# A macaron block on one core: PSUM split into whole-width and small banks, seeds written by ScalarE, and another order at the FFNs' entries

## The chip, the cores and the metric

One core of a Trainium2 chip runs the kernel, in one launch. The metric is the device time of the execution in microseconds; lower is better. The kernel before took 1777.3 us (median of 1776.07, 1777.52 and 1777.30).

Its engines, by the short names of the profile: PE (TensorE) multiplies and accumulates into PSUM, eight banks of 128 x 512 fp32; DVE (VectorE) and ACT (ScalarE) do elementwise work; SP (SyncE) issues the weight loads; POOL (GpSimd) does next to nothing here.

## What is computed

A decoder block on 256 rows of width 2048: half a SwiGLU FFN (hidden width 5632), a token mixer, another half FFN, all fp32, each behind an RMS norm.

```python
x = x + 0.5 * swiglu_ffn(rms_norm(x, ffn1_norm), ffn1_w_gate, ffn1_w_up, ffn1_w_down)
z = rms_norm(x, mix_norm) @ w_in              # 2048 -> 5120
...                                           # y: gated recurrence, gated short convolution
x = x + y @ w_out
x = x + 0.5 * swiglu_ffn(rms_norm(x, ffn2_norm), ffn2_w_gate, ffn2_w_up, ffn2_w_down)
return rms_norm(x, final_norm)

def swiglu_ffn(x, w_gate, w_up, w_down):
    return (silu(x @ w_gate) * (x @ w_up)) @ w_down
```

## The kernel before

Weights come from HBM in units of 512 x 512 (1 MB, `raw_*`, three buffers). For fp32 accuracy each unit is split in two: `hi` is an ACT cast (two of 128x1024), `lo` the DVE difference of raw and hi (one of 128x2048). Activations are split alike. A product then takes three matmuls for each pair of 128-row tile and 128-deep slice: hi by hi and hi by the activation's lo (one group), then the weight's lo by the activation's hi. A unit against one 128-row tile is 12 matmuls of 128x512.

**Order.** A tile scheduler orders each engine's instructions by priorities and dependences; only the opening and the last product are pinned to program order. Each engine runs its queue in that order, and an instruction that waits holds up all that are behind it on its engine.

**The FFN** (`ffn`). The first 512 columns of gate and up are plain products over four units (names `ps_g`, `ps_u`; in FFN1 the gate's is `opening`, made while x arrives). The squares of x are summed meanwhile; `factor` then makes the row factor `r`, and `rows` spreads it: `diag_n` (identity by r) is multiplied by ones into bank `pb_n`, twice, and copied to `bc_n`. Gate and up of the first columns are scaled by r when evicted. For the other columns the normalised activations themselves are made: `v` is hi + lo of the transposed x, times `bc_n`, and is split again into `x` (hi, lo). Sums and differences of its quarters (`seven_of`) give the split `xs`.

The other 5120 columns run as five pairs of gate and up, each a Strassen-Winograd form (`seven`): seven products of half size in place of eight, with one more stream of usual products accumulated in the same banks. A seven has four banks, `a`, `c`, `e` and `d`. Its start: product 0 into `a`, ACT copies `a` to SBUF (`s1`); product 4 into `c`, ACT copies `c` to SBUF (`s5`); then usual products into `e` (fresh) and `c`; product 5 goes on in `a`, and so on. At the end DVE adds the kept copies to the banks, four adds, and the results are `u3`, `u2`, `a` and `s1`. The matmuls of a seven with two streams are 180. Its raw units w11 and w12 are in the `kept` buffers, two, which the two `v` tiles use before them.

After pairs 0, 2 and 4 the hidden units made so far are transposed on PE (`ph`, in `turn_hidden`, called by `settle`), split by ACT (hi) and DVE (lo), some copied back by ACT, and multiplied by the down weights: columns 0 and 3 as plain products (`ps_d`), columns 1 and 2 as a seven. DVE adds half of each result to `xres`, the residual, in SBUF.

**The mixer** projects by w_in (`columns`, `ps_in`), runs the two branches, and projects back by w_out (`ps_o`); DVE adds the result, times a row factor, to `xres`.

**PSUM.** One pool of eight banks serves everything in turn.

**Queues.** SP issues all weight loads in order; a load waits until its buffer is free.

Of the kernel before, what the change touches and what calls it, by code (L numbers as in the profile page):

```python
# [10 lines left out]
F32 = mybir.dt.float32  # L11
# [16 lines left out]
EPS = 1e-6  # L28
SQRT_FLOOR = 2.0**-114


# [17 lines left out]
def hybrid_block(ctx: ExitStack, tc: tile.TileContext, a: dict, out: bass.AP):  # L49
# [28 lines left out]
    work = ctx.enter_context(tc.tile_pool(name="work", bufs=2))  # L78
    psum = ctx.enter_context(tc.tile_pool(name="psum", bufs=8, space=bass.MemoryType.PSUM))

    def bank(name):
        return psum.tile([P, 512], F32, tag="ps", name=name)

# [13 lines left out]
    ones = const.tile([P, P], F32, name="ones")  # L97
    dve.memset(ones, 1.0)
    vec = {}

    def load_vectors(group, name, engine):
        n = sum(g[2] for g in group)
        rows = const.tile([n, P], F32, name=f"rows_{name}")
        cols = const.tile([P, n], F32, name=f"cols_{name}")
        at = 0
        for key, ap, k in group:
            engine.dma_start(rows[at : at + k, :], ap.rearrange("(r p) -> r p", p=P))
            vec[key] = cols[:, at : at + k]
            at += k

        def turn():
            pv = bank(f"pv_{name}")
            pe.transpose(pv[:, :n], rows, ident[:n, :n])
            dve.tensor_copy(cols, pv[:, :n])

        return turn

    first_turn = load_vectors([("ffn1_norm", a["ffn1_norm"][0], 16)], "first", nc.sync)
    load_x(0)
# [87 lines left out]
    class Norm:  # L207
# [12 lines left out]
        def turn(self, ks):  # L220
            for k in ks:
                pt = bank(f"pt_{self.name}_{k}")[:, :S]
# [20 lines left out]
        def rows(self):  # L243

            pb = bank(f"pb_{self.name}")
# [39 lines left out]

    def product(w, c, us, y, name, stagger=False, between=None):
        ps = [bank(f"ps_{name}_{t}") for t in range(NT)]
        cs = slice(c * CW, (c + 1) * CW)
        late = []
        for i, u in enumerate(us):  # L290
            blk = unit(w[u * UK * P : (u + 1) * UK * P, cs], f"{name}_{u}")
            begin, end = i == 0, i == len(us) - 1
            if stagger and i >= len(us) - 2:
                late.append((u, blk, begin, end))
            else:
                multiply([(ps[t], stationary(y(u), t), begin, end) for t in range(NT)], blk)
            if between:
                between(i)
            pump(1.5)
        for t in range(NT):  # L300
            for u, blk, begin, end in late:
                multiply([(ps[t], stationary(y(u), t), begin, end)], blk)
        return ps
# [22 lines left out]
    def seven(w, rows, c0, sf, xs, name, keep, between=None):  # L326
# [50 lines left out]
        product_of(1, w21, d)  # L377
        dve.tensor_tensor(u3, u3, s5, op=ALU.add)
        dve.tensor_tensor(u3, e, u3, op=ALU.add)
        dve.tensor_tensor(u2, c, u2, op=ALU.add)  # L380
        dve.tensor_tensor(s1, d, s1, op=ALU.add)
        return {(1, 1): u3, (0, 1): u2, (1, 0): a, (0, 0): s1}

    def ffn(tag, norm, after, opening=None):
        with tc.tile_pool(name=f"ffn{tag}", bufs=1) as fp:
# [40 lines left out]
            norm.factor()  # L426
            norm.rows()
            sg = [keep(f"sg{tag}_0_{t}") for t in range(NT)]
# [5 lines left out]
            vs = [vs[u // 2][:, :, u % 2, :] for u in range(4)]  # L434
            bcs = norm.bc.unsqueeze(1).to_broadcast([P, UK, S])
            xs = []
            for u in range(4):
                x = f32(norm.xT[u])
# [5 lines left out]
                if u == 1:  # L444
                    pair = [big(f"xs{tag}_{i}") for i in range(2)]
                    sf = seven_of(
                        xs[0], xs[1], {(t, i): vs[i][:, :, t * P : (t + 1) * P] for t in range(NT) for i in range(2)},
                        quad(keep(f"spare{tag}")),
                        [(b[:, :, o : o + P], b[:, :, o + P : o + S]) for b in pair for o in (0, S)],
                    )  # L450
# [9 lines left out]
            def down(last):  # L460
                us = sorted(set(hidden) | {w[0] for w in waiting})

                def update(c, t, ps):
                    xr = xres[:, t, c * CW : (c + 1) * CW]
                    Engine.pinned = last and tag == 2 and c == NC_D - 1
                    dve.scalar_tensor_tensor(xr, ps, 0.5, xr, op0=ALU.mult, op1=ALU.add)
                    if last:
                        after(c, t)

                for c in (0, 3):  # L470
                    end = last and tag == 2 and c == NC_D - 1
                    ps = product(
                        wd, c, us, hidden.get, f"d{tag}_{us[0]}_{c}", end, (lambda i: settle()) if c == 0 else None
                    )
                    for t in range(NT):
                        update(c, t, ps[t])
                    if c == 0:
# [8 lines left out]
                        for c1 in (1, 2):  # L486
                            for t in range(NT):
                                update(c1, t, q[t, c1 - 1])
                hidden.clear()
                turned.clear()  # L490

            for s in range(5):
                c0 = CW + 2 * s * CW
                g = seven(wg, (0, 1), c0, sf, xs, f"g{tag}_{s}", keep, settle)
                for q in ((1, 1), (0, 1), (1, 0), (0, 0)):
                    if q == (1, 0):
                        z = keep(f"z{tag}_{s}")
                        act.activation(z, g[q], AF.Silu)
                        g[q] = z
                    else:  # L500
                        act.activation(g[q], g[q], AF.Silu)
                h = seven(wu, (0, 1), c0, sf, xs, f"u{tag}_{s}", keep)
                for t, n in ((1, 1), (0, 1), (1, 0), (0, 0)):
                    dve.tensor_tensor(g[t, n], h[t, n], g[t, n], op=ALU.mult)
                    waiting.append((1 + 2 * s + n, t, g[t, n], s % 2 == 0))
# [4 lines left out]

    def small(name):
        return const.tile([P, NH], F32, name=name)

    sp2, hba, hbi = small("sp2"), small("hba"), small("hbi")

    def prepare():
# [3 lines left out]
        lam = vec["lru_lambda"]  # L520
        m, e, den, sr, s2, pl = (small(f"lam_{n}") for n in ("abs", "exp", "den", "s", "s2", "poly"))
        act.activation(m, lam, AF.Abs)
# [19 lines left out]
    def opening(wg):  # L542

        ps = [bank(f"ps_g1_0_{t}") for t in range(NT)]
        for u in range(KD // UK):
# [5 lines left out]
            else:  # L551
                blk = unit(src, f"g1_0_{u}")
            for j in range(UK):
# [28 lines left out]

    with tc.tile_pool(name="mixer", bufs=1) as mp, tc.tile_pool(name="mixw", bufs=2) as mw:
        wgate = {}
# [37 lines left out]
        def gates(q):  # L622
# [5 lines left out]
            for g, hb in (("a", hba), ("i", hbi)):  # L628
                hi, lo = wgate[g]
                pg = bank(f"pgate_{g}_{q}")  # L630
                pe.matmul(pg[:, :S], hi[:, q, :], xs[:, :S], start=True, stop=False)
# [149 lines left out]
        for c in range(NC_D):  # L781
            cs = slice(c * CW, (c + 1) * CW)
            for g in range(2):
# [3 lines left out]
                if c == 0:  # L787
                    pst = bank(f"pst_{g}")
                    for t in range(NT):
# [57 lines left out]

    ffn(2, n2, last)

# [29 lines left out]
```

## Time and profile before

| | us |
|---|---|
| median of three runs | 1777.30 |
| profiled execution | 1779.27 |
| its span (first to last instruction) | 1777.3 |
| mean granted clock of PE | 0.994 |

| stage | from about (us) | to about (us) |
|---|---|---|
| FFN1, start to the first seven | 0 | 72 |
| FFN1, sevens and down products | 72 | 736 |
| mixer | 736 | 1059 |
| FFN2, start to the first seven | 1059 | 1109 |
| FFN2, sevens, down products and end | 1109 | 1777 |

How to read the profile: its page has the busy time of each engine. A view of waits sums, for each engine, the idle time before an instruction by what ended it. A timeline lists groups of like instructions by start, with their length, engine, tiles (out <- in), count (xN) and, in brackets, the idle time before them and what ended it. A view of windows has, for each stretch, its length, the busy time of each engine, the granted clock, the share of DMA and GB/s. Names lack buffer numbers: `ps_g` is any of several. All helper calls stand at line 42. Records of matmuls are pipelined: their pitch from start to start, not their length, is what PE needs for one.

### The profile page before, as it was taken

How to read it: one execution, taken by the hardware profiler on the slowest of the kernel's cores; microseconds unless marked ns; L12 is line 12 of the kernel's file. 1: busy time of each engine (PE TensorE's matmuls, PEld its weight loads, DVE VectorE, ACT ScalarE, POOL GpSimd, SP SyncE). 2: the span in 40 equal slices, each digit the busy share in tenths (PEclk: the TensorE clock that was granted, in tenths of full speed). 3: DMA queues.
4: the chain of work that ended last, by engine and by line, in shares of the span. 5: the costliest groups of instructions: out<-in, count | busy, mean ns of one | idle time of the engine just before them, and what ended most of it. 6: DMA issues, size and time to landing. Idle time of an engine off the chain costs nothing. (4 is left out here: it accounts for less than half of the span.)

```text
span 1777.3 us, 20302 instructions
## 1 busy us (share of the span) xinstructions
PE 1744.6 (98%) x8031; PEld 1441.5 (81%) x8031; DVE 1494.4 (84%) x1221; ACT 1046.8 (59%) x1342; POOL 6.9 (0%) x32
## 2 busy tenths in 40 slices
PE   7999999999999999999999999999999999999998
PEld 5787888888888888888888887887888888888886
DVE  6898989989789888688987667989899887899895
ACT  6565556656465656575765554656566664556664
POOL 1000000000000000000000000000000000000000
PEclk9999999999999999999999999999999999999999
DMA  7366655574566574456565655574566637555743
GB/s 249 132 214 212 213 189 190 190 245 155 186 196 209 172 256 166 145 188 196 175 196 170 209 189 190 190 242 157 192 214 202 209 135 259 189 190 190 257 158 106
DMA packets 173905, 343.24 MB, mean 193 GB/s; under 512 B 5621, under 2 KB 8049, under 8 KB 173681
## 3 DMA queue, kind: packets, MB, share of 16 engines
q1 hardware_dynamic: 173344, 340.82, 57.2%
q8 instruction: 63, 1.03, 0.2%
q10 hardware_dynamic: 144, 1.05, 0.2%
q14 instruction: 34, 0.27, 0.0%
q0 software_dynamic: 320, 0.07, 0.0%
HBM read 339.82 MB, written 2.10 MB: 192 GB/s over the span
## 5 line engine op out<-in xcount | busy, mean ns | idle before, releaser
L42 PE MATMUL ps_in<-xT_nm,hi_in 128*128 128x512 f32 x640 | 224.1, 395 | 0.0
L42 ACT CAST hi_g_p<-raw_g 128x1024 fp32r<-128x1024 f32 x140 | 140.5, 1048 | 123.4 <-DVE raw_g L42 40.9
L42 DVE TENSOR_TENSOR lo_g_p<-raw_g,hi_g_p 128x2048 fp32r<-128x2048 f32 x70 | 159.7, 2287 | 36.0 <-ACT hi_g_p L42 35.5
L42 ACT CAST hi_u_p<-raw_u 128x1024 fp32r<-128x1024 f32 x140 | 141.5, 1049 | 66.3 <-PE ps_u_a L42 25.9
L42 PE MATMUL ps_in<-xT_nm,lo_in 128*128 128x256 f32 x640 | 178.6, 281 | 0.6 <-DVE lo_in L42 0.6
L42 DVE TENSOR_TENSOR lo_u_p<-raw_u,hi_u_p 128x2048 fp32r<-128x2048 f32 x70 | 159.2, 2286 | 22.2 <-ACT hi_u_p L42 22.1
L42 PE MATMUL ps_d<-hi_d,h 128*128 128x512 f32 x704 | 172.2, 396 | 2.8 <-DVE h L42 2.2
L42 PEld LDWEIGHTS ps_d<-hi_d,h 128*128 128x128 f32 x704 | 132.6, 189 | 33.3 <-DVE h L42 3.0
L42 PEld LDWEIGHTS ps_in<-xT_nm,hi_in 128*128 128x128 f32 x640 | 119.8, 187 | 27.1
L42 ACT CAST hi_d<-raw_d 128x1024 fp32r<-128x1024 f32 x88 | 88.0, 1048 | 81.9 <-PE ps_u_d L42 25.3
L42 DVE TENSOR_TENSOR lo_d<-raw_d,hi_d 128x2048 fp32r<-128x2048 f32 x44 | 100.7, 2289 | 31.7 <-ACT hi_d L42 31.7
L42 PEld LDWEIGHTS ps_in<-xT_nm,lo_in 128*128 128x128 f32 x640 | 120.6, 189 | 1.4 <-DVE lo_in L42 1.1
L42 DVE TENSOR_TENSOR lo_in<-raw_in,hi_in 128x2048 fp32r<-128x2048 f32 x40 | 91.4, 2285 | 32.7 <-ACT hi_in L42 32.5
L42 ACT CAST hi_in<-raw_in 128x1024 fp32r<-128x1024 f32 x80 | 81.5, 1049 | 62.1 <-PE ps_in L42 48.8
L42 ACT CAST hi_d_p<-raw_d 128x1024 fp32r<-128x1024 f32 x84 | 84.5, 1048 | 48.2 <-DVE raw_d L42 21.0
L42 DVE TENSOR_TENSOR lo_d_p<-raw_d,hi_d_p 128x2048 fp32r<-128x2048 f32 x42 | 95.5, 2287 | 18.9 <-ACT hi_d_p L42 18.8
L42 ACT CAST hi_g_x<-raw_g 128x1024 fp32r<-128x1024 f32 x80 | 80.8, 1049 | 41.2 <-PE ps_g_c L42 19.9
L42 ACT CAST hi_u_x<-raw_u 128x1024 fp32r<-128x1024 f32 x80 | 80.6, 1049 | 37.3 <-PE ps_u_c L42 25.8
L42 DVE TENSOR_TENSOR raw_u<-raw_u,raw_u 128x2048 f32<-128x2048 f32 x40 | 91.6, 2291 | 9.4 <-DMA raw_u<-in_ffn_w_up_dram 8.7
L42 DVE TENSOR_TENSOR raw_g<-raw_g,raw_g 128x2048 f32<-128x2048 f32 x40 | 91.5, 2287 | 6.4 <-DMA raw_g<-in_ffn_w_gate_dram 5.8
L42 DVE TENSOR_TENSOR lo_g_x<-raw_g,hi_g_x 128x2048 fp32r<-128x2048 f32 x40 | 91.4, 2286 | 3.8 <-ACT hi_g_x L42 3.7
L42 DVE TENSOR_TENSOR lo_u_x<-raw_u,hi_u_x 128x2048 fp32r<-128x2048 f32 x40 | 91.5, 2287 | 3.7 <-ACT hi_u_x L42 3.1
(349 smaller groups left out, 3612.5 us busy)
## 6 DMA issues: line engine op xcount, KB each, us to landing
raw_u<-in_ffn_w_up_dram SPq DMA_DIRECT2D x88, 1024.0 KB, 5.3
raw_d<-in_ffn_w_down_dram SPq DMA_DIRECT2D x88, 1024.0 KB, 5.1
raw_g<-in_ffn_w_gate_dram SPq DMA_DIRECT2D x87, 1024.0 KB, 5.3
raw_in<-in_w_in_dram SPq DMA_DIRECT2D x40, 1024.0 KB, 5.1
raw_o<-in_w_out_dram SPq DMA_DIRECT2D x16, 1024.0 KB, 5.1
xres<-in_x_dram SPq DMA_DIRECT2D x4, 512.0 KB, 8.3
fin<-in_final_norm_dram ACTq DMA_DIRECT2D x1, 1024.0 KB, 4.7
out_dram<-xres SPq DMA_DIRECT2D x4, 256.0 KB, 2.7
```

Of the source, the lines that this page charges most:

```text
L42: ins = getattr(self.engine, name)(*args, **kwargs)
```

## The change

- PSUM: in each FFN six banks ("full") for products and two ("part") for transposes and other small results; all eight in the mixer for both. The pools are opened for FFN1, the mixer and FFN2 in turn, over the same banks. When an FFN's pools are opened, six matmuls on zeros write the six full banks (`first_*`).
- Sevens: after product 0 ACT copies `a` to bank `d`, and after product 4 `c` to bank `e`; the later products accumulate on them, with no start flag. Two of four DVE adds go; the other two are made where the result is used.
- Down products, columns 0 and 3 (all but the very last): ACT writes twice the residual into the bank first, the matmuls accumulate on it, and ACT writes half of the bank to `xres`.
- Opening: units 1 to 3 of FFN1's first product have their lo made in two halves.
- Row factor: `rows` and the normalising of unit u are called from within the up product (`between=normalise`), after its unit u, and not ahead of that product.

```diff
+    zeros = const.tile([P, 512], F32R, name="zeros")
+    dve.memset(f32(zeros), 0.0)
...
+    def banks(name, parts):
+        with ExitStack() as st:
+            for kind, n in (("full", 8 - parts), ("part", parts)):
+                if n:
+                    pools[kind] = st.enter_context(
+                        tc.tile_pool(name=f"{kind}_{name}", bufs=n, space=bass.MemoryType.PSUM)
+                    )
+            if parts:
+                for i in range(8 - parts):
+                    pe.matmul(bank(f"first_{name}_{i}"), zeros[:, :P], zeros, start=True, stop=True)
+            else:
+                pools["part"] = pools["full"]
+            yield
...
+    def small(name):
+        return bank(name, "part")
...
-    def product(w, c, us, y, name, stagger=False, between=None):
+    def product(w, c, us, y, name, stagger=False, between=None, base=None):
         ps = [bank(f"ps_{name}_{t}") for t in range(NT)]
+        if base:
+            for t in range(NT):
+                act.activation(ps[t], base(t), AF.Copy, scale=2.0)
...
-            begin, end = i == 0, i == len(us) - 1
+            begin, end = i == 0 and not base, i == len(us) - 1
...
         product_of(0, w11, a, True)
-        s1 = snap(a, "s1")
+        act.copy(d, a)
         dve.tensor_tensor(w11, w12, w11, op=ALU.subtract)
         product_of(4, w11, c, True)
-        s5 = snap(c, "s5")
-        usual(0, b2, 1, (e, 1, True, not two), (c, 0, False, False))
+        act.copy(e, c)
+        usual(0, b2, 1, (e, 1, False, not two), (c, 0, False, False))
...
-        usual(0, a2, 0, (d, 0, True, False), (a, 1, False, False))
+        usual(0, a2, 0, (d, 0, False, False), (a, 1, False, False))
...
-        dve.tensor_tensor(u3, u3, s5, op=ALU.add)
-        dve.tensor_tensor(u3, e, u3, op=ALU.add)
-        dve.tensor_tensor(u2, c, u2, op=ALU.add)
-        dve.tensor_tensor(s1, d, s1, op=ALU.add)
-        return {(1, 1): u3, (0, 1): u2, (1, 0): a, (0, 0): s1}
+        return {(1, 1): (e, u3), (0, 1): (c, u2), (1, 0): (a, None), (0, 0): (d, None)}
...
-                pt = bank(f"ph{tag}_{u}_{t}")
+                pt = small(f"ph{tag}_{u}_{t}")
...
             norm.factor()
-            norm.rows()
...
-            for u in range(4):
+
+            def normalise(u):
+                if u == 0:
+                    norm.rows()
+                bcs = norm.bc.unsqueeze(1).to_broadcast([P, UK, S])
                 x = f32(norm.xT[u])
                 dve.tensor_tensor(vs[u], x[:, :, :S], x[:, :, S:], op=ALU.add)
                 dve.tensor_tensor(vs[u], vs[u], bcs, op=ALU.mult)
...
+            pu = product(wu, 0, range(4), norm.xT.__getitem__, f"u{tag}_0", between=normalise)
             xs = list(enumerate(xs))[2:]
-            pu = product(wu, 0, range(4), norm.xT.__getitem__, f"u{tag}_0")
...
                     ps = product(
-                        wd, c, us, hidden.get, f"d{tag}_{us[0]}_{c}", end, (lambda i: settle()) if c == 0 else None
+                        wd, c, us, hidden.get, f"d{tag}_{us[0]}_{c}", end, (lambda i: settle()) if c == 0 else None,
+                        None if end else lambda t: columns_of(c, t),
                     )
...
+                        xr = columns_of(c, t)
+                        if end:
+                            Engine.pinned = True
+                            dve.scalar_tensor_tensor(xr, ps[t], 0.5, xr, op0=ALU.mult, op1=ALU.add)
+                        else:
+                            act.activation(xr, ps[t], AF.Copy, scale=0.5)
...
-                blk = unit(src, f"g1_0_{u}")
+                halves_of = ((0, 2), (2, 4))
+                blk = parts_of(load(src, f"g1_0_{u}"), f"g1_0_{u}", halves_of, lambda i: None)
...
+    ffn1_banks.close()
-    with tc.tile_pool(name="mixer", bufs=1) as mp, tc.tile_pool(name="mixw", bufs=2) as mw:
+    with tc.tile_pool(name="mixer", bufs=1) as mp, tc.tile_pool(name="mixw", bufs=2) as mw, banks("mixer", 0):
...
-    ffn(2, n2, last)
+    with banks("ffn2", 2):
+        ffn(2, n2, last)
```

In a seven, the gate's and up's epilogues add `e` to `u3` and `c` to `u2` on DVE and read `a` and `d` from PSUM directly; in the down product the two parts are added to `xres` one after the other.

More of the change, by code (lines that the diff above doesn't have):

```diff
@@ L2 @@
 from collections import deque
-from contextlib import ExitStack
+from contextlib import ExitStack, contextmanager
 import concourse.bass as bass
@@ L29 @@
 SQRT_FLOOR = 2.0**-114
+QUADS = ((1, 1), (0, 1), (1, 0), (0, 0))
 class Engine:
@@ L78, in hybrid_block, with bank @@
     work = ctx.enter_context(tc.tile_pool(name="work", bufs=2))
-    psum = ctx.enter_context(tc.tile_pool(name="psum", bufs=8, space=bass.MemoryType.PSUM))
-    def bank(name):
-        return psum.tile([P, 512], F32, tag="ps", name=name)
+    pools = {}
+    @contextmanager
+    def banks(name, parts):
[11 more added lines that the diff above has]
+            yield
+    def bank(name, kind="full"):
+        return pools[kind].tile([P, 512], F32, tag="ps", name=name)
+    def small(name):
+        return bank(name, "part")
     def f32(ap):
@@ L111, in turn @@
         def turn():
-            pv = bank(f"pv_{name}")
+            pv = small(f"pv_{name}")
             pe.transpose(pv[:, :n], rows, ident[:n, :n])
@@ L221, in turn @@
             for k in ks:
-                pt = bank(f"pt_{self.name}_{k}")[:, :S]
+                pt = small(f"pt_{self.name}_{k}")[:, :S]
                 for t in range(NT):
@@ L243, in rows @@
         def rows(self):
-            pb = bank(f"pb_{self.name}")
+            pb = small(f"pb_{self.name}")
             for t in range(NT):
@@ L295, in product @@
             else:
-                multiply([(ps[t], stationary(y(u), t), begin, end) for t in range(NT)], blk)
+                multiply([(ps[t], stationary(y(u), t), begin, end) for t in range(NT)], blk, base is not None)
             if between:
@@ L301, in product @@
             for u, blk, begin, end in late:
-                multiply([(ps[t], stationary(y(u), t), begin, end)], blk)
+                multiply([(ps[t], stationary(y(u), t), begin, end)], blk, base is not None)
         return ps
@@ L461, in down, with columns_of @@
                 us = sorted(set(hidden) | {w[0] for w in waiting})
[L463 to L468, printed above, removed]
+                def columns_of(c, t):
+                    return xres[:, t, c * CW : (c + 1) * CW]
                 for c in (0, 3):
@@ L487, in down @@
                             for t in range(NT):
-                                update(c1, t, q[t, c1 - 1])
+                                xr = columns_of(c1, t)
+                                for part in q[t, c1 - 1]:
+                                    if part is not None:
+                                        dve.scalar_tensor_tensor(xr, part, 0.5, xr, op0=ALU.mult, op1=ALU.add)
+                                if last:
+                                    after(c1, t)
                 hidden.clear()
```

44 lines of the change are left out of this document (26 added, 18 removed).

## The prediction

> **What bounds the kernel now.** I read the totals of the page first, then PE's waits, then the granted clock in the stretches around the largest of them.
>
> ```profile
> span 1777.3 us, 20302 instructions
> PE 1744.6 (98%) x8031; PEld 1441.5 (81%) x8031; DVE 1494.4 (84%) x1221; ACT 1046.8 (59%) x1342; POOL 6.9 (0%) x32
> ```
>
> PE is busy for 98% of the span, DVE for 84%. What an edit on DVE or ACT can win is what PE waits for them:
>
> ```profile
> PE ps_g L42 <- DVE lo_g L42: 5.2, 3, 2.0
> PE pb_n L42 <- DVE diag_n L42: 4.5, 1, 4.5
> PE ps_u L42 <- DVE lo_u L42: 2.6, 1, 2.6
> PE ps_d L42 <- DVE h L42: 2.2, 2, 1.1
> PE ps_g_c L42 <- ACT hi_g_p L42: 1.6, 1, 1.6
> ```
>
> Columns: who waited for whom, total us, how often, the longest. These five sum to 16.1 us. All sit at the two FFNs' entries or, the fourth, at their first down products; none is in the 20 full gate and up Strassen products after the entry. Shorter DVE work inside those can win nothing by itself: u_0 runs its products without a gap, as the next rows show.
>
> ```profile
> 121.60 1.08 PE L42 MATMUL ps_u_c<-lo_u_p,xs 128*128 128x512 f32 x4
> 122.52 2.01 PE L42 MATMUL ps_u_e<-hi_u_x,x 128*128 128x512 f32 x8
> ```
>
> From start to start of these two groups 4 matmuls take 0.92 us: a pitch of 0.23 us (so the last of them lasts 1.08 - 3 x 0.23 = 0.39). Some entry waits also cost clock:
>
> ```profile
> 25.00:35.30 10.30, 6.65 (x33) 5.26 (x33) 6.76 (x7) 6.47 (x14) 0.00 (x0) 1.00 0.33 103
> 35.90:39.30 3.40, 3.40 (x10) 2.66 (x9) 2.66 (x4) 3.38 (x8) 0.00 (x0) 0.50 0.75 252
> 46.50:53.00 6.50, 6.36 (x16) 4.94 (x17) 4.63 (x6) 2.14 (x3) 0.00 (x0) 0.50 0.53 161
> ...
> 1097.00:1104.30 7.30, 4.75 (x15) 3.44 (x14) 5.61 (x4) 1.88 (x2) 0.00 (x0) 0.77 0.83 289
> ...
> 62.00:82.00 20.00, 18.38 (x81) 14.38 (x80) 15.86 (x17) 9.52 (x12) 0.00 (x0) 1.00 0.45 158
> ```
>
> The column after POOL is the granted clock. It is 0.50 for 3.4 us after a wait of 2.0 us in the opening, which costs half of that, 1.7 us of work, and for 6.5 us after the wait of 4.5 for diag, 3.3; around the wait for lo_u its mean is 0.77 over 7.3 us, 1.7. It stayed 1.00 from 62 to 82 us, in spite of the 1.6 us wait for hi_g_p there. So waits of about a microsecond cost only themselves.
>
> **The change part by part.** The sum is made against the profiled span, 1777.3 us.
>
> *Copies between banks (e from c).* Before, when product 4 ended in bank c, ACT copied c to SBUF while PE went on in a fresh bank e. Now e is filled by ACT from c, and e's first matmul waits for it. The nearest rows are the old copy and the one place where PE did wait for it:
>
> ```profile
> 1116.34 1.18 PE L42 MATMUL ps_g_c<-lo_g_p,xs 128*128 128x512 f32 x4
> 1117.55 0.58 ACT L42 COPY s_g<-ps_g_c 128x512 f32<-128x512 f32 x1 [0.35 <-PE ps_g_c L42]
> 1118.19 1.21 PE L42 MATMUL ps_g_c<-hi_g_x,x 128*128 128x512 f32 x4 [0.24 <-ACT s_g L42]
> ```
>
> The last of the four matmuls starts 0.39 before 1117.52, at 1117.13; ACT starts 0.42 later, copies for 0.58, and PE goes on 0.06 after. So e begins 1.06 us after c's last matmul begins instead of 0.23: a stall of 0.83, and 0.9 where ACT is in the middle of a cast. In PE's new order e follows c directly in 16 of the 26 Strassen products; in six, four matmuls of another product (0.91 us) stand between, in four, seven, and there the copy is covered. Without the two of g_0, which belong to the entries below, 14 x 0.87 = 12.2 us. The trace has no ACT write into PSUM. From below: with a copy of no length the stall is 0.25, 3.5 us in all; from above, the 0.63 us of ACT's SBUF row further down gives 0.92, 12.9 us. I take the copy's own row, for it reads the same bank and has the same shape. The copy d from a is used much later and costs nothing while ten or more matmuls cover it.
>
> The Trainium skill, ScalarE: Activation LUTs (Step-by-step: what each stage is for), says that ScalarE writes PSUM sooner than SBUF; no row here shows such a write. It gives no figure; by it the sum would lie between the two ends above.
>
> *New pools at FFN2.* Its banks lie over the mixer's, so six matmuls on zeros come first and the first waits until the last w_out bank is read.
>
> ```profile
> 1059.49 2.29 DVE L42 TENSOR_TENSOR lo_g<-raw_g,hi_g 128x2048 fp32r<-128x2048 f32 x1 [2.53 <-ACT hi_g L42]
> 1059.68 3.79 PE L42 MATMUL ps_g<-hi_g,xT_n 128*128 128x512 f32 x16
> 1061.70 1.40 DVE L42 SCALAR_TENSOR_TENSOR xres<-ps_o,r_y,xres 128x512 f32<-128x512 f32 x2
> ```
>
> Before, ps_g began at 1059.68 in other banks while DVE did lo_g, and only then read ps_o, until 1063.10. DVE's order here is unchanged, so PE stands still for 1063.1 - 1059.7 = 3.4 us, and the six matmuls take 1.4: 4.8. If lo_g were not in front, 1.1; with a cold clock after it, 6.5. At the kernel's start the same six lie before x has landed, and cost nothing.
>
> *Mixer.* Its first matmul now waits for ACT's eviction of the last ps_d bank.
>
> ```profile
> 735.83 0.69 DVE L42 SCALAR_TENSOR_TENSOR xres<-ps_d,xres 128x512 f32<-128x512 f32 x1 [1.39 <-PE ps_d L42]
> ...
> 736.55 0.40 PE L42 MATMUL ps_in<-xT_nm,hi_in 128*128 128x512 f32 x1
> 736.62 0.63 ACT L42 ACTIVATE junk_nm<-xres 128x512 f32<-128x512 f32 x1 [4.46 <-DVE xres L42]
> ```
>
> On ACT stand now an eviction (0.6 by the copy's row, from 735.8 like DVE's), a square of 0.63 with 0.19 to read its sum, and then the eviction waited for, 0.6: about 737.9 against 736.55, +1.35. Other edits that move evictions from DVE to ACT (22, with 22 base writes) lie under down products and cost nothing; so do the 73 DVE operations taken away, about 0.69 each (50 us). If ACT's 44 at 0.6 (26 us) weren't covered, they would come after casts whose matmuls PE has not reached; ACT has 41% to spare.
>
> *Opening and row factor, FFN1.*
>
> ```profile
> 31.66 1.23 DVE L42 TENSOR_TENSOR v<-xT_n 128x1024 f32<-128x1024 f32 x1
> ...
> 35.30 0.50 PE L42 MATMUL ps_g<-lo_g,xT_n 128*128 128x512 f32 x1 [2.01 <-DVE lo_g L42]
> 46.64 0.76 PE L42 MATMUL pb_n<-diag_n,ones 128*128 128x128 f32 x2 [4.47 <-DVE diag_n L42]
> 67.22 2.00 ACT L42 CAST hi_g_p<-raw_g 128x1024 fp32r<-128x1024 f32 x2 [6.44 <-DMA raw_g<-in_ffn_w_gate_dram]
> 72.59 2.11 PE L42 MATMUL ps_g_a<-hi_g_p,x 128*128 128x512 f32 x8
> ```
>
> Three lo subtractions are halved; the row of a 128x1024 operation says 1.23 in place of 2.29, so each of the three waits (5.2) shrinks by 1.1: 3.2, and with the cold stretch 1.7: g_0's plain product ends 4.9 earlier. pb now comes after 24 matmuls of ps_u (5.5 us of cover, 37.3 + 5.5 = 42.8); diag, 46.6 before, comes some 2 us earlier with the lo's ahead of it, and the wait shrinks to about 1.6, its 3.3 of cold clock with it. But what follows doesn't move with it: the raw weights of the first Strassen product share two buffers with v, so their load is issued when the normalising work is over and lands at 67.2. That work starts from bc, which on DVE now stands behind one lo_u more, and begins only 0.6 us earlier. PE's 11 us (4.9 + 2.9 + 3.3) become idle time before 72.59, when hi, lo and difference of the first units must be made with nothing else to run. I put the net at +0.5, between -0.7 (the load's gain kept) and +2 (cold clock).
>
> *FFN2's entry.* Same edit, without an opening to win. The first row is of the page's DMA issues (KB each, us to landing).
>
> ```profile
> raw_g<-in_ffn_w_gate_dram SPq DMA_DIRECT2D x87, 1024.0 KB, 5.3
> ```
>
> ```profile
> 1082.61 0.71 PE L42 MATMUL ps_u<-hi_u,xT_n 128*128 128x512 f32 x2
> 1083.76 0.43 DVE L42 COPY bc_n<-pb_n 128x256 f32<-128x256 f32 x1 [0.58 <-PE pb_n L42]
> 1096.99 1.22 DVE L42 TENSOR_TENSOR x<-v,x 128x1024 fp32r<-128x1024 f32 x1
> 1100.46 3.47 PE L42 MATMUL ps_u<-lo_u,xT_n 128*128 128x512 f32 x8 [2.55 <-DVE lo_u L42]
> 1102.42 1.99 ACT L42 CAST hi_g_p<-raw_g 128x1024 fp32r<-128x1024 f32 x2 [6.50 <-DMA raw_g<-in_ffn_w_gate_dram]
> 1106.78 2.29 DVE L42 TENSOR_TENSOR raw_g<-raw_g,raw_g 128x2048 f32<-128x2048 f32 x1
> 1109.45 2.01 PE L42 MATMUL ps_g_a<-hi_g_p,x 128*128 128x512 f32 x8
> ```
>
> Before, normalising began 1.2 us after ps_u's start U (1082.6), delayed lo_u by 2.55 us and chilled the clock (1.7), but let the load land before U + 19.8. Now all four lo_u stand ahead: hi of the fourth waits for the first unit's 16 matmuls (3.8), then cast 2.0, lo 2.3, diag and pb 1.2, copy 0.4: bc at U + 9.7. Normalising takes 14 us as before (1083.8 to 1098.2) and ends at U + 23.7, where PE has ended ps_u, 96 x 0.227 = 21.8. The load, issued at U + 22.7, needs 5.3 us: U + 28.1. Cast 1.0, lo 2.3, difference 2.3, casts 2.0, lo 2.3 and the exposed copy follow one on the other, while each product holds only 2.7 us of matmuls. Walked through to the end of the third product (5), PE ends at U + 49.2, against 36.7 without a wait: 12.5 lost, where the same stretch lost 5.6 before: +6.9. From below +5 (loads landing sooner), from above +12 (the idle stretches cold).
>
> *Two banks for transposes.* At each FFN's first down product the transposes had eight banks; now the third pair waits for copies out of the first.
>
> ```profile
> 164.11 2.29 DVE L42 TENSOR_TENSOR lo_d_p<-raw_d,hi_d_p 128x2048 fp32r<-128x2048 f32 x1 [2.09 <-ACT hi_d_p L42]
> 166.32 2.48 DVE L42 TENSOR_TENSOR h<-ph,h 128x512 fp32r<-128x512 f32 x4
> 167.04 1.18 ACT L42 COPY u_g<-ph 128x512 f32<-128x512 f32 x2 [0.65 <-DVE h L42]
> 168.26 5.05 PE L42 MATMUL ps_d<-hi_d,h 128*128 128x512 f32 x14 [1.08 <-DVE h L42]
> ```
>
> DVE is in lo_d_p until 166.3; then lo of h, ACT's copy out (167.0 to 167.6), the third transposes, their cast, and on DVE a raw difference of 2.3 ahead of their lo: PE is back at 170.5 to 171.1 instead of 168.26. +2.6 each, 5.2. If the difference were not ahead, 0.3 each.
>
> Sum: 12.2 + 4.8 + 1.35 + 0.5 + 6.9 + 5.2 = 31, so 1808 us. The profiled run's span equals the median of the runs shown, 1777.3, so it stands for that median.
>
> **The rivals.**
> *Entries win (other side).* Place: PE between the last matmul of ps_u and the first of g_0. If those raw weights land before ps_u ends, nothing takes the place of the old waits: 5.2 + 4.5 + 2.6 + 1.6 = 13.9 and 6.7 of cold clock (1.7 + 3.3 + 1.7) are won, 20.6 in place of the 7.4 lost. It decides from a landing before U + 21.8. With the seams at their lower end, 4.0 for all sixteen, and 11.4 for boundaries and transposes: 1772; with mine, 14.0, 1782. For it: 16 us of waits are real. Against: the shared buffers and DVE's order. 11 in 100 for not slower this way.
>
> *Seams only.* DVE has 5% less to do; if that lets the entries come out even and the transposes too, copies and boundaries alone remain: 14 + 6.1 = 20, 1797. Against: at the places named, the order puts the same 2.3 us subtractions ahead. 22 in 100.
>
> *Cold after seams.* Every exposed copy halves the clock for 3.4 us: 16 x 1.7 = 27 more, 1835. Against: the stretch 62 to 82 us above, with a longer wait and no loss of clock. 5 in 100. TensorE: Matmul & The Clock Gate in the Trainium skill (A second HAM failure mode: psum-queue depth-cycling) has this rule: frequent micro-idles of PE between banks make the gate swing.
>
> *Cold entries.* The idle stretches of FFN2's entry, its boundary and its first down product are each followed by 1.7, and FFN2's entry takes its upper end: 1808 + 5.1 + 3.4 = 1816 or 1817. For it: 0.50 after 2.0 us. 17 in 100.
>
> **How the numbers follow.** The forecast has 45 in 100 (about 1800 to 1815), the rivals the rest: 11, 22, 5, 17. The range from 1784 to 1822 leaves out the first rival's lower end and the cold seams, some 2 in 10 with what I haven't thought of. Differences under 0.2% (3.6 us) can't be told from none. Faster 0.08, same 0.03, slower 0.89, all of the first two from the first rival.
>
> **What would show it.** PE's waits would name ps_g_e, ps_u_e and ps_d_e after ACT, 16 times, about 0.6 to 0.7 us of idle each by the profile's reckoning; first_ffn2 after DVE for some 3 us; ps_g_a at both entries after ACT hi_g_p or DVE for several us; ph after ACT. The DVE total would fall by about 50 us with no gain in the steady stretches. I am wrong if PE's rows show e beginning within 0.5 us of c's last matmul, if g_0's first matmul stands under U + 24, or if the steady u_0 takes under 41 us.

## The result, and the profile after

The changed kernel takes 1823.95 us (median of four runs, 1823.43 to 1825.07) against 1777.41 before: a ratio of 1.0254, 95% interval 1.0227 to 1.0282. The profiled execution has a span of 1822.0 us, 44.7 more than before. The forecast was 1808, with a range up to 1822: the direction was right, the loss half as large again as worked out, and the time lies outside the range.

Totals of the page and PE's waits, after (who waited for whom, total us, how often, the longest):

```profile
span 1822.0 us, 20316 instructions
PE 1763.7 (97%) x8043; PEld 1444.4 (79%) x8043; DVE 1460.3 (80%) x1151; ACT 1071.8 (59%) x1386; POOL 6.9 (0%) x32
```

```profile
PE ps_u_e L43 <- ACT ps_u_e L43: 6.9, 10, 0.7
PE ph L43 <- ACT u_g L43: 5.9, 2, 2.9
...
PE pt_n L43 <- DVE xT_n L43: 3.5, 5, 0.9
PE first_ffn L43 <- DVE xres L43: 3.1, 1, 3.1
PE ps_g_e L43 <- ACT ps_g_e L43: 2.7, 2, 1.4
PE ps_d_e L43 <- ACT ps_d_e L43: 2.6, 4, 0.7
PE ps_d_c L43 <- DVE lo_d_p L43: 2.3, 1, 2.3
...
PE ps_d_c L43 <- ACT hi_d_p L43: 1.7, 1, 1.7
```

DVE lost 34 us of busy time and PE won nothing by it. (About 50 was forecast. The lengths of the operations on DVE add up to 47.5 less; the busy total falls by less, since records that stand back to back overlap.) The waits of before for lo_g, diag_n and lo_u have all but gone, and those above stand in their place. As forecast, PE waits 16 times for a copy into bank e, once for the zeros of FFN2 and twice for ph. The waits for pt_n and the two for ps_d_c the prediction does not name.

The times below are starts of PE's stretches in the traces, each from its first matmul to the next stretch's. A "seven" is one Strassen-Winograd product; g_0 and u_0 are the first gate and up sevens, d_5 and d_9 the down sevens after pairs 2 and 4. "Cold" means at a granted clock below 1.

| stretch | before | after | more | forecast |
|---|---|---|---|---|
| FFN1: to the first gate matmul | 7.67 | 9.13 | 1.46 | |
| FFN1: first gate product | 39.39 | 31.08 | -8.31 | |
| FFN1: first up product | 25.53 | 28.93 | 3.40 | |
| FFN1: g_0 | 44.44 | 51.93 | 7.49 | |
| these four | | | 4.0 | 0.5 |
| 14 sevens with an exposed copy (all u, d_5, d_9) | | | 13.2 | 12.2 |
| first down product, FFN1 and FFN2 | 42.94 | 46.67 | 3.7 | 5.2 |
| into the mixer | | | 1.4 | 1.35 |
| w_out to FFN2's first gate matmul | 90.69 | 96.52 | 5.8 | 4.8 |
| FFN2: first gate, first up, g_0 | 92.71 | 100.65 | 7.9 | 6.9 |
| FFN2: last seven (d_9), beyond its copy | 41.92 | 47.55 | 5.6 | 0 |
| all others | | | 2.9 | 0 |
| sum | | | 44.6 | 31 |

### The profile page after: what moved, and what is told of

It is laid out like the page before. It is cut to its first block, busy times and chain, and to the rows that moved or that the text cites. A ratio compares the mean times of both kernels' runs of the same rounds, so it can differ in the third digit from the quotient of the medians.

```text
span 1822.0 us, 20316 instructions
## 1 busy us (share of the span) xinstructions
PE 1763.7 (97%) x8043; PEld 1444.4 (79%) x8043; DVE 1460.3 (80%) x1151; ACT 1071.8 (59%) x1386; POOL 6.9 (0%) x32
## 4 chain that ended last, share of the span: by engine, by line
PE 90%; DVE 4%; ACT 3%; DMA 2%; issue 1%; DVEq 0%; SPq 0%; ACTq 0%
PE ps_d L43 12%; PE ps_in L43 12%; PE ps_u_a L43 9%; PE ps_g_a L43 9%; PE ps_g_c L43 6%; PE ps_u_c L43 6%; PE ps_d_a L43 5%; PE ps_u_d L43 5%; PE ps_g_d L43 5%; PE ps_o L43 4%; PE ps_d_c L43 3%; PE ps_g_e L43 3%; PE ps_u_e L43 3%; PE ps_d_d L43 2%; PE ps_g L43 2%; PE ps_d_e L43 2%
## 5 line engine op out<-in xcount | busy, mean ns | idle before, releaser
L43 ACT CAST hi_d_p<-raw_d 128x1024 fp32r<-128x1024 f32 x84 | 85.9, 1050 | 55.3 <-PE ps_d_a L43 20.1
```

The costliest lines, as they stand in the source:

```text
L43: ins = getattr(self.engine, name)(*args, **kwargs)
```

## The experiments

All spans are of profiled executions; before has 1777.3, after 1822.0. Where no more runs are named there is one, and fifteen executions of the kernel before in one session lay between 1775.3 and 1781.9 us: a difference of two or three microseconds in a span can't be told from none, and single stretches are read instead. In e8 to e11 transposes share banks with seeded sums, and these kernels no longer give the block's output (lost seeds are the likely reason; no run isolates it). They show where time goes and are no replacements.

**e1: the copies back in SBUF**

```diff
-        act.copy(d, a)
+        s1 = snap(a, "s1")
...
-        act.copy(e, c)
-        usual(0, b2, 1, (e, 1, False, not two), ...
+        s5 = snap(c, "s5")
+        usual(0, b2, 1, (e, 1, True, not two), ...
...                                           # d likewise begun afresh; DVE adds s5 and s1
```

> The changed kernel (span 1822.0 us) with ACT's copies of a and c going to SBUF again and e and d begun afresh by matmuls. Theory (each exposed copy costs its own stall): the 14 u- and d-products that start e right behind c each lose 0.92 to 1.01 us in the changed kernel, so 13.4 us come back, and about 1 more at each FFN's g_0: span 1806 to 1809. PE's waits for ps_u_e, ps_d_e and ps_g_e on ACT are gone. Rival (the wait moves on: DVE has its four adds again, and another late lo takes the place of the copy): under 5 us come back, 1817 to 1822.

Measured: 1800.1, 21.9 less. The ten u sevens and d_5 are back at their old length (41.18 for u_0, which took 42.15); g_0 gives back 3.8 in FFN1 and 1.5 in FFN2. The last seven, not expected, falls from 48.47 to 43.95. The theory of the stalls holds and its rival falls; the span lies 6 us below the theory's range, because g_0 and the last seven give back more than it had.

**e4: the copy covered.** The same copies, but product 0's four lo matmuls into `a` come after product 4.

```diff
-        product_of(0, w11, a, True)
-        act.copy(d, a)
+        blk = parts_of(w11, f"{name}_p0")
+        ...                                   # product 0, hi matmuls only
         dve.tensor_tensor(w11, w12, w11, op=ALU.subtract)
         product_of(4, w11, c, True)
         act.copy(e, c)
+        ...                                   # product 0, its four lo matmuls
+        act.copy(d, a)
```

> The changed kernel with the four lo matmuls of product 0 moved behind product 4, so that 0.9 us of matmuls into a stand between the last into c and the first into e; same operations. Theory (the stall is the latency of the copy, 0.92 to 1.01, less one pitch): it is covered, the waits for ps_u_e and ps_d_e fall to under 0.2 each, and 11 to 14 us come back: 1808 to 1811. Rival (the copy is late because ACT is, or the stall only moves to c, which the copy reads, or to the d copy, now later): under 6 us, 1816 to 1822.

Measured: 1807.9, 14.1 less. The timeline of PE and ACT in the changed kernel at u_0, then of PE in e4:

```profile
125.64 1.08 PE L43 MATMUL ps_u_c<-lo_u_p,xs 128*128 128x512 f32 x4
125.84 1.05 ACT L43 CAST hi_u_x<-raw_u 128x1024 fp32r<-128x1024 f32 x1 [1.28 <-PE ps_u_c L43]
126.80 0.58 ACT L43 COPY ps_u_e<-ps_u_c 128x512 f32<-128x512 f32 x1
...
127.43 2.11 PE L43 MATMUL ps_u_e<-hi_u_x,x 128*128 128x512 f32 x8 [0.71 <-ACT ps_u_e L43]
```

```profile
121.86 1.08 PE L43 MATMUL ps_u_c<-lo_u_p,xs 128*128 128x512 f32 x4
122.78 1.10 PE L43 MATMUL ps_u_a<-lo_u_p,x 128*128 128x512 f32 x4
123.71 2.04 PE L43 MATMUL ps_u_e<-hi_u_x,x 128*128 128x512 f32 x8
```

In the first, e starts 1.79 us after the start of c's group of four, and the wait is the copy. In the second, four matmuls fill that time: 1.85 from c to e, which is eight matmuls at a pitch of 0.23 (1.84), and no idle time. ACT does the same copies. So the copies cost what their place exposes. The last seven is not helped (48.52).

**e2: base and eviction of the down products back on DVE**

```diff
-                        None if end else lambda t: columns_of(c, t),
...
-                            dve.scalar_tensor_tensor(xr, ps[t], 0.5, xr, op0=ALU.mult, op1=ALU.add)
-                        else:
-                            act.activation(xr, ps[t], AF.Copy, scale=0.5)
+                        dve.scalar_tensor_tensor(xr, ps[t], 0.5, xr, op0=ALU.mult, op1=ALU.add)
```

> The changed kernel with the plain down products begun by a matmul and added to the residual by DVE, as before; nothing else changed. Theory (evictions and squares on ACT hold up the casts of the last Strassen product of FFN2, which lost 6.55 us against 0.93 in its like of FFN1's pair 2): 5 to 6 us come back there, 0.9 before the mixer, and about 0.4 in FFN1's last: span 1814 to 1816. Rival (the loss there comes from the exposed copy and the two transpose banks): the last Strassen product stays within 1.5 us of the changed kernel's, span 1819 to 1822.

Measured: 1823.7, 1.7 more. The last seven takes 49.04: the theory falls, evictions on ACT are at most a small part of its loss. PE waits 4.1 us in it, 0.6 less, at a granted clock of 0.93 for 0.96. (The squares stay on ACT in e2, so they are not cleared.) The mixer's first stretch is 1.5 shorter (231.43 for 232.94). FFN1's first gate product is 2.0 longer (33.04), with no edit near it and the same operations in the same order on PE, DVE and ACT: the matmuls come 0.43 us apart until 18.2 us, where in the changed kernel's run they come 0.23 apart from 14.2 on. A stretch can so differ by 2 us between two runs of the same instructions.

**e3: the normalising back ahead of the first up product**

```diff
             norm.factor()
+            norm.rows()
...
-                if u == 0:
-                    norm.rows()
...
-            pu = product(wu, 0, range(4), norm.xT.__getitem__, f"u{tag}_0", between=normalise)
+            for u in range(4):
+                normalise(u)
+            pu = product(wu, 0, range(4), norm.xT.__getitem__, f"u{tag}_0")
```

> The changed kernel with the row factor spread and the activations normalised ahead of the first up product, as before, for both FFNs; nothing else changed. Theory (the late normalising delays the load of the first raw weights of g_0, because they share buffers with v): PE waits 4 to 5 us for pb in FFN1 again, but g_0 starts with its loads there; FFN2's stretch from its up product to u_0 gives back 6 to 8 us, FFN1's 3 to 6: span 1808 to 1813. Rival (g_0 is held by the exposed copy and its lo's, not by the load): under 3 us in all, 1819 to 1825.

Measured: 1821.9. In FFN1 nothing moves (31.08, 28.99, 51.99): the scheduler had put pb and the lo's of ps_u in the same order from either place. In FFN2 the up product is 26.85 again, with its wait for lo_u of 2.55, and g_0 falls to 46.17: 4.3 back. FFN2's first down product, 2.0 longer, and the last seven, 1.7 longer (50.20), give nearly all of it away. Both ran colder than in the changed kernel's run (granted clock 0.72 for 1.00 from 1230 to 1240 us, 0.93 for 0.96 in the last seven). By its span the run lies in the rival's range. By the stretches the theory holds for FFN2, for half of what that entry loses, and not for FFN1.

**e6: the opening's lo's whole again**

```diff
-                halves_of = ((0, 2), (2, 4))
-                blk = parts_of(load(src, f"g1_0_{u}"), f"g1_0_{u}", halves_of, lambda i: None)
+                blk = unit(src, f"g1_0_{u}")
```

> The changed kernel with the opening's lo subtractions whole again. Moving the normalising back in program order left FFN1's stretches as they were, so its order there follows from something else. Theory (the earlier end of the opening makes the scheduler put pb and the lo's of ps_u before the normalising): the opening is 39 us again, with pb's wait back, ps_u 25.5 and g_0 within 2 us of 44.4 + 2.8 (its exposed copy): span 1820 to 1823. Rival (the pools do it): opening 39, but ps_u and g_0 still 81 together: 1829 or more.

Measured: 1823.6. From the first gate matmul to u_0 it takes 111.4 us, with the halves 111.9: inside the changed kernel the halves win nothing. Both sides failed: no wait for pb comes back, since PE takes up-product matmuls between the last gate ones.

**e5 and e12: the halves alone, on the kernel before** (the same three lines, the other way round)

> The kernel before with nothing changed but the opening's three lo subtractions in halves. In the changed kernel the first gate product took 31.1 us instead of 39.4, and then the first up product and g_0 together 80.9 instead of 70.0. Theory (what is won in the opening is lost again at g_0 whatever else is changed, because g_0's raw weights wait for buffers of v): the opening wins 8 us here too and the next two stretches lose 5 to 9: span 1774 to 1778. Rival (the loss belongs to the changed kernel's small banks and seeds): the win stays, 1768 to 1771.

> The kernel before with the opening's three lo subtractions in halves alone, timed in rounds: its one look gave a span of 1774.1 against 1777.3. Theory (the opening keeps 3.2 us of what it wins): 0.15 to 0.2% faster than before. Rival (spread of the runs): no difference outside the interval.

Measured: a span of 1774.1 in e5. In e12 five runs have a median of 1773.66 us (1768.71 to 1774.14) against 1779.49 before in the same session, a ratio of 0.9962 with an interval of 0.9949 to 0.9975: 0.4% faster than before, clear of the spread. In e12 the first gate product takes 32.45 for 39.39, ps_u 1.25 less, g_0 3.4 more. PE's waits in e12:

```profile
PE pb_n L42 <- DVE diag_n L42: 3.5, 1, 3.5
...
PE ps_g L42 <- DVE lo_g L42: 1.8, 3, 0.8
```

The three waits for lo_g shrank from 5.2 to 1.8, by 3.4, where 3.2 was worked out. FFN1 reaches u_0 at 113.4 us in e5 and 112.3 in e12, for 117.0 before. About half of the win stays, which lies between the theory (none) and its rival (all).

**e7: the final gain's scaling on GpSimd**

```diff
-                    dve.tensor_scalar(lastgain, lastgain, -0.5, None, op0=ALU.mult)
+                    nc.gpsimd.tensor_scalar(lastgain, lastgain, -0.5, None, op0=ALU.mult)
```

> The changed kernel with one operation moved: the scaling of the last quarter of the final gain runs on GpSimd and not on DVE. In the changed kernel DVE stood 2.58 us in it, waiting for the load of that gain, 10 us before the last Strassen product, which lost 6.55 us (0.9 of it the copy). Theory (DVE's 2.6 us make the first differences late, and ACT then takes other casts first): that stretch falls from 48.5 to 42.8 to 45: span 1816 to 1819. Rival (the order on ACT alone, with the copy d from a ahead of the casts of product 4, does it): 48 or more, 1821 to 1823.

Measured: 1825.6; the last seven 49.46. DVE no longer stands in that wait, and nothing is won: the theory falls, the rival's 48 or more stands. The operation takes 2.94 us on GpSimd.

**e8: one pool of eight banks for everything, no zeros**

> The changed kernel with one pool of eight banks opened once, for everything, and no matmuls on zeros; the seeds and copies between banks stay. Theory (the pools cost the wait and six matmuls before FFN2, ACT's eviction before the mixer, the third pair of transposes at the first down products, and the zeros at the start): 5.8 + 0.9 + 1.5 + 2.2 + 1.4 = about 12 come back: span 1808 to 1812. Rival (with eight shared banks the four of a Strassen product are not free in time, since results stay in PSUM until they are used): PE waits for banks at the starts of products, 1815 or more.

Measured: 1798.0, 24.0 less, twice what was expected. W_out to FFN2 is 90.71 (before 90.69), the first down products 41.4 together (46.67), and the last seven 42.28: its loss beyond the copy is gone. So is FFN1's, and more: u_0 begins at 113.5 us, where it begins at 121.1 in the changed kernel and at 117.0 before. FFN2's entry keeps its loss (100.5 for 100.65).

**e9, e10: transposes back in the whole-width banks**, first those of hidden units (`ph`), then also those of x and the residual (`pt`)

```diff
-                pt = small(f"ph{tag}_{u}_{t}")
+                pt = bank(f"ph{tag}_{u}_{t}")
...
-                pt = small(f"pt_{self.name}_{k}")[:, :S]
+                pt = bank(f"pt_{self.name}_{k}")[:, :S]
```

> The changed kernel with the transposes of the hidden units (ph) in the six whole-width banks; everything else as changed. Theory (with two banks the third and fourth transposes come 3 us later, everything on DVE behind them shifts by 3.6, and in the last down product ACT then casts for product 4 behind evictions and squares): both first down stretches come back to 20.7 to 22.3 (they took 23.8 and 22.9), and the last Strassen product falls from 48.5 to 43 to 44: span 1811 to 1815. Rival (these stretches wait for ACT's seeds and evictions): under 2 us, 1820 to 1823.

> As the kernel with ph in the whole-width banks, and the transposes of x and of the residual (pt) there too. Theory (in the opening PE waits 3.5 us, five times, for DVE and ACT to empty one of two banks of transposes): the opening falls from 31.1 to 28 to 29, as with one pool (28.7), but g_0 gives part of it back, so that the stretch from the first gate matmul to u_0 (112.0) falls by 1 to 3 us; and 0 to 1 us in the mixer. Rival (g_0's raw weights set that stretch): it stays within 0.5 us.

Measured: 1807.3 and 1801.9. With `ph` moved, the first down products take 20.7 each, the last seven 42.28, g_0 of FFN1 48.89. With `pt` moved too, the first gate matmul comes at 7.68 (9.13 in the changed kernel) and the opening falls to 27.70. PE's first rows before, in the changed kernel, and in e10:

```profile
5.91 1.97 PE L42 MATMUL pt_n<-ident,xres 128*128 128x128 f32 x8 [3.21 <-DMA xres<-in_x_dram]
7.67 1.22 PE L42 MATMUL ps_g<-hi_g,xT_n 128*128 128x512 f32 x2
```

```profile
5.91 1.12 PE L43 MATMUL pt_n<-ident,xres 128*128 128x128 f32 x4 [1.18 <-DMA xres<-in_x_dram]
7.69 0.69 PE L43 MATMUL pt_n<-ident,xres 128*128 128x128 f32 x2 [0.66 <-DVE xT_n L43]
8.79 0.69 PE L43 MATMUL pt_n<-ident,xres 128*128 128x128 f32 x2 [0.42 <-DVE xT_n L43]
9.13 1.20 PE L43 MATMUL ps_g<-hi_g,xT_n 128*128 128x512 f32 x2
```

```profile
5.95 1.94 PE L43 MATMUL pt_n<-ident,xres 128*128 128x128 f32 x8 [1.22 <-DMA xres<-in_x_dram]
7.68 1.22 PE L43 MATMUL ps_g<-hi_g,xT_n 128*128 128x512 f32 x2
```

Both theories hold by their mechanism, both rivals fall, and both effects are larger than expected: e9's span is 4 us below its range, and from the first gate matmul to u_0 e10 takes 104.8 us for the changed kernel's 111.9, where 1 to 3 less was expected. With whole-width banks for all transposes 20.1 us of the span come back. By the stretches it is 8.6 up to u_0 (112.5 for 121.1), 5.3 in the two first down products and 6.2 in the last seven; the others nearly cancel. e8, which has no small banks either, gives 7.6, 5.3 and 6.2 back in the same places. The prediction has 5.2 for the two small banks.

How two banks reach a product some 20 us later is to be seen in ACT's and PE's timelines before the last seven, in the changed kernel, and then in e9:

```profile
1742.36 1.04 ACT L43 CAST hi_d_x<-raw_d 128x1024 fp32r<-128x1024 f32 x1
1743.29 0.64 ACT L43 ACTIVATE junk_f<-xres 128x512 f32<-128x512 f32 x1
...
1745.54 0.58 ACT L43 COPY ps_d_d<-ps_d_a 128x512 f32<-128x512 f32 x1
1746.05 1.99 ACT L43 CAST hi_d_p<-raw_d 128x1024 fp32r<-128x1024 f32 x2
...
1747.15 2.15 PE L43 MATMUL ps_d_c<-hi_d_p,hs 128*128 128x512 f32 x8 [1.72 <-ACT hi_d_p L43]
...
1751.63 1.20 PE L43 MATMUL ps_d_c<-lo_d_p,hs 128*128 128x512 f32 x4 [2.34 <-DVE lo_d_p L43]
```

```profile
1730.78 2.00 ACT L43 CAST hi_d_p<-raw_d 128x1024 fp32r<-128x1024 f32 x2 [4.46 <-DVE raw_d L43]
1733.26 0.60 ACT L43 ACTIVATE xres<-ps_d 128x512 f32<-128x512 f32 x1 [0.48 <-PE ps_d L43]
...
1736.75 2.03 PE L43 MATMUL ps_d_c<-hi_d_p,hs 128*128 128x512 f32 x8
```

The rows hi_d_p are the casts for product 4. In e9 they end 4 us before PE wants them. In the changed kernel the transposes come later, the Strassen sums of the hidden units and the first difference of raw weights with them, and ACT's order has other casts, evictions, squares and the copy d from a first; PE stands 1.7 us for the cast and 2.3 for its lo, and then runs cold. The small banks are not enough by themselves: with them, but with the copies going to SBUF, this seven took 43.95 (e1), two of the 6.5 us lost. Windows of the changed kernel after long waits of PE:

```profile
1751.60:1758.00 6.40, 5.71 (x17) 4.22 (x18) 4.33 (x2) 4.46 (x5) 0.00 (x0) 0.73 0.37 142
169.10:176.00 6.90, 3.96 (x19) 2.33 (x17) 6.72 (x6) 3.73 (x7) 0.00 (x0) 0.83 0.33 128
72.00:80.00 8.00, 4.81 (x16) 2.86 (x14) 8.00 (x11) 4.47 (x6) 0.00 (x0) 0.83 0.00 0
1075.00:1082.00 7.00, 3.93 (x10) 3.15 (x11) 6.52 (x12) 2.92 (x7) 0.00 (x0) 0.76 0.78 261
1230.00:1237.00 7.00, 3.80 (x17) 2.41 (x18) 7.00 (x7) 4.16 (x8) 0.00 (x0) 1.00 0.22 85
```

The column after POOL's is the granted clock. It is below 1 in the first four. In the last PE waited 2.94 us for ph in FFN2, as long as in its twin of FFN1 (the second row), and the clock stayed 1.00. So a wait of that length mostly costs clock here, but not each time.

**e11: the remedies together.** One pool, zeros in all eight banks at the start, the covered copy, the normalising ahead.

> One pool of eight banks opened once, zeros written into all eight at the start while x is loaded; the copy into e covered by the four lo matmuls of product 0; normalising ahead of the first up product as before; seeds by ACT and halved opening as changed. Theory (the terms add): 1798 with one pool, less 13 to 14 for the copies, less 2.7 in FFN1's g_0 and 4 in FFN2's: span 1776 to 1781, the kernel before at 1777. Rival (with shared banks the seeds come late): 1785 or more.

Measured: a span of 1774.9; in ten runs 1779.17 against 1779.49 before, ratio 1.0004, interval 0.9994 to 1.0014. The theory holds: the loss of 2.5% is gone, as a sum. Not each term is: FFN2's entry still takes 95.8 us for 92.7 before, and FFN1, with its halved opening, reaches u_0 3.5 earlier than before (113.5). What fewer DVE operations and seeds by ACT are worth by themselves is not shown; no gain of theirs is left to see.

## Why the prediction failed

The mechanisms named were there, but one of them was looked for in one place only; by the spans the sum was short by 13.6 us.

- *Two banks for transposes: the step that failed.* "At each FFN's first down product the transposes had eight banks; now the third pair waits for copies out of the first": the prediction costed the two banks there alone, at 5.2, and put nothing for every other place that transposes. e10 puts them at about 20: 5.3 at the first down products, 8.6 up to FFN1's u_0, 6.2 in the last seven.
- *Last seven: +5.6 beyond its copy, for 0.* Without it the time would lie inside the range. e7 clears the gain's load and e2 all but clears the evictions, so "lie under down products and cost nothing" nearly holds for these; e9 shows the two transpose banks, by way of ACT's order, and e1 shows that the copies into banks are needed for most of it too. The cause was at hand, only its other places were missed.
- *FFN1 to u_0: +4.0 for +0.5.* Two misses of opposite sign. The transposes of x in two banks were not costed at all: PE waits 3.5 us for pt_n, and 1.46 of that delay stands before the first gate matmul. The six matmuls on zeros at the kernel's start cost nothing, as forecast: the first transposes start at 5.91 us with and without them. On the other side, PE's time won in the opening does not all "become idle time before 72.59": g_0 began at 69.15, and with whole-width banks u_0 comes 4.5 earlier than before (e10). The copy in g_0 has no price of its own in that sum; e1 gives back 3.8 there, since PE has nothing else to do there and runs cold (granted 0.50 from 82 to 88 us). "Begins only 0.6 us earlier" of the normalising was wrong too: bc came at 49.52, 0.9 later than before.
- *Copies: +13.2 for 12.2.* Right. The stall was 0.91 to 1.01 a time; ACT's copy into PSUM took 0.58, the same as the row chosen.
- *FFN2's pools: +5.8 for 4.8.* Right in place: PE waited 3.07 for the old banks. The six matmuls took 2.6 and not 1.4, cold, the case the prediction priced at 6.5:

```profile
1076.61 1.41 DVE L43 SCALAR_TENSOR_TENSOR xres<-ps_o,r_y,xres 128x512 f32<-128x512 f32 x2
...
1078.07 2.81 PE L43 MATMUL first_ffn<-zeros 128*128 128x512 f32 x6 [3.07 <-DVE xres L43]
...
1080.67 2.69 PE L43 MATMUL ps_g<-hi_g,xT_n 128*128 128x512 f32 x9
```

- *FFN2's entry: +7.9 for 6.9.* The walk held. From U, the start of ps_u at 1104.03, bc was forecast at U + 9.7 and its copy ended at U + 9.35, and g_0's first matmul, forecast at U + 29.1 (28.1 and a cast of 1.0), came at U + 28.6. Of the 7.9, the late normalising is 4.3 (e3) and the copy in g_0 1.5 (e1):

```profile
1112.96 0.42 DVE L43 COPY bc_n<-pb_n 128x256 f32<-128x256 f32 x1 [0.58 <-PE pb_n L43]
```

```profile
1132.65 3.76 PE L43 MATMUL ps_g_a<-hi_g_p,x 128*128 128x512 f32 x8 [3.21 <-ACT hi_g_p L43]
```

- *Mixer: 1.4 for 1.35.* In part luck: at the boundary it is 0.9, with PE waiting 1.0 for ACT's xres as forecast. The other 0.5 lies in the mixer's first stretch, which took 229.8 to 234.5 us in the runs here.
- *First down products: 3.7 for 5.2*, PE waiting 2.94 in each for ACT's copy out of the first bank: the path that was named.
- *Small ones, 2.9.* Sevens with "covered" copies still cost 0.1 to 0.2, and down products at pairs 2 and 4 a quarter of a microsecond each.
- *Rivals.* Entries did not win. The cold clock after seams did not come: u_0 runs at full clock (granted 1.00 from 121 to 163 us) in spite of its stall of 0.7, as argued from the 1.6 us wait. The rule in TensorE: Matmul & The Clock Gate of the Trainium skill (A second HAM failure mode: psum-queue depth-cycling), that frequent micro-idles make the clock swing, does not show with one idle of 0.7 us in 42. Cold entries did come, if not at FFN2's first down product, and 1816 was the nearest case. The prediction's "0.50 after 2.0 us" was one of two: its own row of 25 to 35.3 us has 1.00 after an equal wait at 26.6.

In ScalarE: Activation LUTs (Step-by-step: what each stage is for), the Trainium skill has ScalarE quicker into PSUM than into SBUF. From SBUF that agrees: the base writes took 0.593 us (median of 22), where ACT's casts and squares of the same shape within SBUF took 0.62 to 0.63, though these are other operations. From PSUM no difference shows: 0.577 for the copy of `c` into bank `e`, 0.580 for the old copy into SBUF.

Partly open: why the halved opening keeps 3.6 to 4.8 us up to u_0 on the kernel before and nothing inside the changed one. The two small banks are the likely reason: with all transposes in whole-width banks u_0 comes at 112.5 us (e10), as in e12 (112.3). No run has whole subtractions and whole-width banks together, so this is argued and not shown. Half of the opening's win is lost at g_0 in both kernels; more buffers for its raw weights were not run.

## What to carry to other kernels

When a pool is split, follow every kind of tile that now shares the smaller part through the whole program, last occurrence included, and not only the place where the wait was first found. Here a copy that seeds a running sum cost next to nothing once four matmuls stood between its source's last and its target's first (u_0 took 41.22 us for 41.18); that reordering was worth more than the operations saved. On a kernel that is 98% PE, look for the PE wait that names an operation before taking it off DVE: three halved subtractions that PE waited for won 0.4%, while no gain of the seventy removed operations shows in any run.

## What the runs showed that was not expected

- An order written in the program did not decide: with a scheduler between, moving the normalising left FFN1's order as it was (e3).
- The same instructions in the same order took 2.0 us longer in another run's opening (e2), because the matmuls came 0.43 us apart for some 4 us longer. One run's difference of that size in one stretch says nothing of an edit.
- Six matmuls of 128x512 on zeros took 0.43 each after an idle time of 3.07 us, against 0.23 in the steady stretches, so a wait and the work behind it must be costed together.
